# Five direct tiles instead of three, and input combinations on VectorE, in a seven-product feed-forward stage

## The chip, the cores and the metric

One core of one Trainium2 chip. The metric is the device time of one execution in microseconds (us); the kernel before has a median of 2582.3 us over 3 runs (2580.14 to 2583.24).

## The reference, cut to what matters

Four feed-forward stages (two layers, two in each) take most of the time. With `h` the normalised input (1024 features, 512 tokens) each computes

```python
def swiglu(h, w_gate, w_up, w_down):        # 1024 -> 2816 -> 1024
    return (jax.nn.silu(h @ w_gate) * (h @ w_up)) @ w_down
x = x + 0.5 * swiglu(rms_norm(x, norm), w_gate, w_up, w_down)
```

All of it is float32. The kernel gets that precision by splitting each operand into a high part, rounded to a short format (`fp32r`), and a low part (operand minus high part), and adds three products of parts: high by high, high by low, low by high.

## The kernel before

Everything is held with features on the 128 partitions and the 512 tokens along the free dimension, so `h` is 8 blocks of 128x512. The 2816 hidden features are 22 tiles of 128, numbered `f` = 0 to 21. `ffn` (line 340) runs `up(f)` for each tile, which gives the product of gate and up for those 128 features, split into `gh`/`gl`, and `down(k, ...)` for each of 8 output blocks and each chunk of tiles. `CHUNKS` puts the tiles 0 to 3 into the first chunk, 4 to 7 into the second, and so on. The 8 `down` calls of a chunk are spread over the tiles of the next: two after each `up`.

A tile is computed in one of two ways.

- **Direct** (`direct`, line 227; the tiles below `DIRECT`, here 0, 1 and 2): 8 blocks x 3 products of parts x 2 matrices = 48 matmuls of 512 columns on the unscaled input `xh`/`xl`; the result is multiplied by the normalisation factor `R` when it leaves PSUM (lines 238 and 241).
- **Seven products** (`winograd`, line 305; the tiles from 3 on): a scheme of Strassen's kind on 2x2 blocks, with 7 products of 256 columns instead of 8: 7 x 4 x 3 = 84 matmuls of 256 columns. It needs combinations of the weights (`blocks`, line 272: four sums, two on GpSimd and two on VectorE, then splits of seven 128x512 pieces, line 299 on ScalarE and line 300 on VectorE) and combinations of the scaled input (`forms`, line 244: once for each stage).

`forms` needs `R`, which is the broadcast of the input's norm (line 129, on VectorE) and comes late in the direct tiles. For each of four pairs of input blocks it scales two blocks on VectorE (line 253, into tiles `gh3`, `gl3`), makes four differences of 128x256 on GpSimd (line 260, into tiles of the tags `cu` and `s`, of which there are two each; `direct` and `winograd` put their own results `u` and `s` into the same tags), copies seven 128x256 high parts on ScalarE (line 267, `fh`) and subtracts for the low parts on VectorE (line 268, `fl`), in pieces of 256, 512, 512 and 512 columns.

What sets the order. The kernel is written in Tile. The order of each engine's instructions is fixed when the program is built: whenever an engine comes free in its own time model, a planner takes the instruction that stands earliest in the program among those that are ready there. `high_priority(offset=100)` around `weights` and `blocks` lets these count as 100 instructions earlier. `forms` is written between `up(0)` and `up(1)`; in the third stage, which follows the end of the first layer, `late` (lines 214 to 222) comes right behind it: a broadcast and eight scalings of `x` (line 220). A direct tile is 60 instructions. Tiles of one tag rotate through its buffers in program order, so a new one waits until the one that many places before is no longer used. The weights' raw data has two buffers (`raw`), their parts three each (`whi`, `wlo`); a direct tile takes two of each, a `down` one, a seven-product tile four of `whi`/`wlo`. Its raw blocks go into tiles that are free at the time: for `f` = 3 into `gh4` to `gl7`, for later ones into the slots of the input blocks `xh0` to `xl7`, which the direct tiles still read. PSUM has three banks of tag `s`, three of `t`, two of `acc`.

## Time and profile before

| | us |
|---|---|
| median of 3 runs | 2582.3 |
| the profiled execution | 2590.04 |
| its span, from the first to the last instruction | 2588.3 |
| busy: TensorE matmul / weight load | 2438.3 / 2114.6 |
| busy: VectorE / ScalarE / GpSimd | 1877.3 / 1293.1 / 814.9 |
| mean granted clock of TensorE | 0.970 |

The page gives busy time by engine and by line, the views of the trace each instruction with its start, its duration and what ended the idle time before it. PE is TensorE's matmuls, PEld its weight loads, DVE VectorE, ACT ScalarE, POOL GpSimd, SP the engine that issues the DMAs. A matmul's duration runs from its start to its modelled end and overlaps with the next, so the rate is read from the distance of two starts.

### The profile page before, as it was taken

To read this page: it belongs to the slowest core of one execution; us is meant where nothing else is said; L and a number is where in the kernel's file an instruction comes from. 1 tells how busy PE (TensorE), PEld (TensorE's weight loads), DVE (VectorE), ACT (ScalarE), POOL (GpSimd) and SP (SyncE) were. 2 spreads that over 40 slices of the span, in tenths; PEclk is the share of its full clock that TensorE was granted. 3 is DMA by queue.
4 is the path that set the end of the run, shared out by engine and by line. 5 is a ranking of instruction groups with operands and counts; after the bars stand their busy time and mean duration, and the time that the engine had idled before them with its cause. 6 is when DMAs were issued, how large, how long until landed. Compare 5 with 4: busy or idle time off the path is not lost. (4 is left out here: it accounts for less than half of the span.)

```text
span 2588.3 us, 40395 instructions
## 1 busy us (share of the span) xinstructions
PE 2438.3 (94%) x15192; PEld 2114.6 (82%) x15192; DVE 1877.3 (73%) x3307; ACT 1293.1 (50%) x2494; POOL 814.9 (31%) x647
## 2 busy tenths in 40 slices
PE   6999999999979999979999999999899998889998
PEld 5899988886669999769999888767799997777867
DVE  8877776976588777698777689755977766755444
ACT  4444456676444444544444576764444445334544
POOL 5212115652341111441211447224312104442312
PEclk8999999999989999989999999999899999999989
DMA  5233333211223332323332432012233324220111
GB/s 161 78 106 103 96 111 108 84 50 34 84 69 102 103 105 78 103 70 103 100 105 70 129 103 80 19 52 87 93 103 100 105 61 144 63 80 25 40 45 56
DMA packets 117284, 220.58 MB, mean 85 GB/s; under 512 B 22544, under 2 KB 33872, under 8 KB 117088
## 3 DMA queue, kind: packets, MB, share of 16 engines
q1 hardware_dynamic: 113680, 217.68, 27.7%
q8 instruction: 119, 1.95, 0.3%
q10 hardware_dynamic: 3408, 0.33, 0.1%
q14 instruction: 77, 0.63, 0.1%
HBM read 209.14 MB, written 8.78 MB: 84 GB/s over the span
## 5 line engine op out<-in xcount | busy, mean ns | idle before, releaser
L292 POOL TENSOR_TENSOR xl<-xh,xh 128x512 f32<-128x512 f32 x144 | 212.8, 1479 | 834.7 <-DVE wlo L300 458.9
L88 ACT ACTIVATE whi<-raw 128x512 fp32r<-128x512 f32 (+4 forms) x327 | 246.1, 754 | 433.5 <-PE t L317 222.4
L317 PE MATMUL t<-fl,whi 128*128 128x256 f32 x1216 | 342.6, 282 | 8.8 <-DVE fl L268 8.8
L317 PE MATMUL t<-fh,whi 128*128 128x256 f32 x1216 | 342.5, 282 | 6.2 <-ACT fh L267 6.2
L317 PE MATMUL t<-fh,wlo 128*128 128x256 f32 x1216 | 342.3, 281 | 1.0 <-DVE wlo L300 1.0
L99 PE MATMUL acc<-gh,whi 128*128 128x512 f32 x704 | 278.6, 397 | 7.8 <-DVE x L370 4.5
L317 PE MATMUL s<-fl,whi 128*128 128x256 f32 x912 | 258.9, 284 | 26.6 <-DVE fl L268 26.6
L101 PE MATMUL acc<-gh,wlo 128*128 128x512 f32 x704 | 278.1, 396 | 0.3
L100 PE MATMUL acc<-gl,whi 128*128 128x512 f32 x704 | 278.2, 396 | 0.0
L317 PE MATMUL s<-fh,whi 128*128 128x256 f32 x912 | 259.0, 284 | 11.4 <-ACT fh L267 8.4
L317 PE MATMUL s<-fh,wlo 128*128 128x256 f32 x912 | 257.1, 282 | 0.2 <-DVE wlo L300 0.2
L317 PEld LDWEIGHTS t<-fl,whi 128*128 128x128 f32 x1216 | 231.4, 190 | 16.1 <-DVE fl L268 9.8
L317 PEld LDWEIGHTS t<-fh,whi 128*128 128x128 f32 x1216 | 231.1, 190 | 13.5 <-ACT fh L267 7.0
L89 DVE TENSOR_TENSOR wlo<-raw,whi 128x512 fp32r<-128x512 f32 (+3 forms) x253 | 204.0, 807 | 50.4 <-ACT whi L88 49.6
L299 ACT ACTIVATE whi<-xh 128x512 fp32r<-128x512 f32 x216 | 136.7, 633 | 207.0 <-issue 113.3
L89 POOL TENSOR_TENSOR wlo<-raw,whi 128x1024 fp32r<-128x1024 f32 (+2 forms) x74 | 167.1, 2259 | 220.4 <-ACT whi L88 206.7
L317 PEld LDWEIGHTS t<-fh,wlo 128*128 128x128 f32 x1216 | 231.5, 190 | 1.4 <-DVE wlo L300 1.4
L300 DVE TENSOR_TENSOR wlo<-xh,whi 128x512 fp32r<-128x512 f32 x216 | 179.3, 830 | 33.3 <-ACT whi L299 33.2
L317 PEld LDWEIGHTS s<-fl,whi 128*128 128x128 f32 x912 | 174.0, 191 | 32.9 <-DVE fl L268 29.6
L299 ACT ACTIVATE whi<-xl 128x512 fp32r<-128x512 f32 x288 | 171.6, 620 | 57.2 <-PE t L317 48.7
L300 DVE TENSOR_TENSOR wlo<-xl,whi 128x512 fp32r<-128x512 f32 x288 | 192.9, 691 | 4.6 <-ACT whi L299 4.6
L317 PEld LDWEIGHTS s<-fh,whi 128*128 128x128 f32 x912 | 174.1, 191 | 17.8 <-ACT fh L267 10.3
(714 smaller groups left out, 6412.4 us busy)
## 6 DMA issues: line engine op xcount, KB each, us to landing
xh<-in_ffn_gu_dram SPq DMA_DIRECT2D x288, 256.0 KB, 2.6
raw<-in_ffn_d_dram SPq DMA_DIRECT2D x128, 256.0 KB, 2.6
raw<-in_w2f_dram SPq DMA_DIRECT2D x25, 512.0 KB, 3.6
raw<-in_ffn_gu_dram SPq DMA_DIRECT2D x24, 512.0 KB, 3.7
raw<-in_ffn_d_dram SPq DMA_DIRECT2D x64, 192.0 KB, 2.4
xs<-x SPq DMA_DIRECT2D x24, 256.0 KB, 2.6
raw<-in_a_dram SPq DMA_DIRECT2D x12, 512.0 KB, 3.5
x<-xs SPq DMA_DIRECT2D x24, 256.0 KB, 2.8
```

The lines of the kernel that those rows point to most:

```text
L88: nc.scalar.activation(out=hi, in_=raw, func=AF.Copy)
L89: (lo_eng or self.lo_eng).tensor_tensor(out=lo, in0=raw, in1=hi.bitcast(F32), op=ALU.subtract)
L99: mm(out=out, lhsT=lh, rhs=rh, start=start, stop=False)
L100: mm(out=out, lhsT=lh, rhs=rl, start=False, stop=False)
L101: mm(out=out, lhsT=ll, rhs=rh, start=False, stop=stop)
L292: eng.tensor_tensor(out=o, in0=x, in1=y, op=op)
L299: nc.scalar.activation(out=hi[:, c], in_=src, func=AF.Copy)
L300: nc.vector.tensor_tensor(out=lo[:, c], in0=src, in1=hi[:, c].bitcast(F32), op=ALU.subtract)
L317: nc.tensor.matmul(out=out, lhsT=x[:, k], rhs=y[:, j], start=start and k == 0 and n == 0, stop=stop and k == 3 and n == 2, skip_group_chec ...
```

## The change

`DIRECT` goes from 3 to 5: the whole first chunk and the first tile of the second are computed directly, and the first seven-product tile is `f` = 5. `forms` makes its four differences on VectorE, into one tile `W` of a new tag `tw` with one buffer, and splits them with one copy and one subtraction of 1024 columns; its two scaled blocks alternate between `gh7`/`gl7` and `gh4`/`gl4`. The raw blocks of the first seven-product tile come as two transfers of 512 KB into the tag `raw` instead of four of 256 KB into pool tiles, and its sums go into `gh5`, `gh6`, `gl5`, `gl6`. Each of the four stages' pools begins with a filler of 0, 8, 16 or 24 floats, so that all its tiles move up by 0, 32, 64 or 96 bytes.

```diff
@@ -56,7 +56,7 @@
         self.nc.sync.dma_start(out=t, in_=ap)
         return t
 
-    BUFS = dict(sqt=2, ms=4, hms=4, rs4=4, rs8=2, r12=2, s=2, cu=2, wu=2, nm=6, sum=6, rsum=6, cms=2, lms=2, lats=2,
+    BUFS = dict(sqt=2, ms=4, hms=4, rs4=4, rs8=2, r12=2, s=2, cu=2, wu=2, tw=1, nm=6, sum=6, rsum=6, cms=2, lms=2, lats=2,
                 beta=2, sq_=1, st=10, p=8, pth=3, ptl=3, vv=2, lat=6, ysq=2, c1=4, sums=3, frs=2, ft=2, fR=2, rr=1, y=4, dup=4, bias=1,
                 t3=4, t15=4, rt=1, kr=4, ahr=4, chr=4, hr=4, shift=2, tmp=3, n4=3, dense=2, L4=2, q4=3, t32t=2, UA=2, SA=2, ST=2, SG=1, yrw=1,
                 rest=2, sbt=3, rwms=2, sig=1, gate=1, oacc=8, fss1=4, fss=4, rs1=4, sums_=1)
@@ -246,26 +246,22 @@
 
         nc = self.nc
         out = []
+        lo, hi = slice(0, 256), slice(256, 512)
+        flat = lambda t: t.rearrange("p e c -> p (e c)")
+        sub = lambda o, x, y: nc.vector.tensor_tensor(out=o, in0=x, in1=y, op=ALU.subtract)
         for k in range(4):
-            hs = []
-            for j, tag in ((k, "gh3"), (k + 4, "gl3")):
-                h = self.t(gp, tag)
-                nc.vector.scalar_tensor_tensor(out=h, in0=self.x[j], scalar=gain[:, j:j + 1], in1=R, op0=ALU.mult, op1=ALU.mult)
-                hs.append(h)
-            a, b = hs
             H, L = self.t(gp, f"fh{k}", (P, 7, 256), F32R), self.t(gp, f"fl{k}", (P, 7, 256), F32R)
-            half = lambda t: t.rearrange("p (e c) -> p e c", e=2)
-            w0, w1 = half(self.t(gp, "cu")), half(self.t(gp, "s"))
-            lo, hi = slice(0, 256), slice(256, 512)
-            sub = lambda o, x, y: nc.gpsimd.tensor_tensor(out=o, in0=x, in1=y, op=ALU.subtract)
-            sub(w0[:, 0], a[:, hi], a[:, lo])
-            sub(w0[:, 1], b[:, hi], w0[:, 0])
-            sub(w1[:, 0], b[:, hi], a[:, hi])
-            sub(w1[:, 1], b[:, lo], w0[:, 1])
-            for j, src in ((0, half(a)[:, 0:1]), (1, half(b)), (3, w0), (5, w1)):
-                n = src.shape[1]
-                nc.scalar.activation(out=H[:, j:j + n], in_=src, func=AF.Copy)
-                nc.vector.tensor_tensor(out=L[:, j:j + n], in0=src, in1=H[:, j:j + n].bitcast(F32), op=ALU.subtract)
+            a, b = (self.t(gp, f"g{e}{7 - 3 * (k % 2)}") for e in "hl")
+            for j, o in ((k, a), (k + 4, b)):
+                nc.vector.scalar_tensor_tensor(out=o, in0=self.x[j], scalar=gain[:, j:j + 1], in1=R, op0=ALU.mult, op1=ALU.mult)
+            W = self.t(gp, "tw", (P, 4, 256))
+            sub(W[:, 0], a[:, hi], a[:, lo])
+            sub(W[:, 1], b[:, hi], W[:, 0])
+            sub(W[:, 2], b[:, hi], a[:, hi])
+            sub(W[:, 3], b[:, lo], W[:, 1])
+            for j, n, src in ((0, 1, a[:, lo]), (1, 2, b), (3, 4, flat(W))):
+                nc.scalar.activation(out=flat(H[:, j:j + n]), in_=src, func=AF.Copy)
+                sub(flat(L[:, j:j + n]), src, flat(H[:, j:j + n]).bitcast(F32))
             out.append((H, L))
         return out
 
@@ -274,17 +270,20 @@
 
         nc = self.nc
         with self.tc.high_priority(offset=self.ahead):
+            A = []
             if f == DIRECT:
-                slots = [(gp, f"g{t}{4 + i}") for t in "hl" for i in range(4)]
+                slot = iter([(gp, f"g{t}{i}") for t in "hl" for i in (5, 6)])
+                for which in range(2):
+                    t = self.wp.tile([P, 1024], F32, tag="raw", name=self.name("raw"), bufs=2)
+                    nc.sync.dma_start(out=t, in_=wgu[f, which])
+                    A += [t[:, 0:S], t[:, S:]]
             else:
-                slots = [(self.xp, f"x{t}{4 * (f % 2) + i}") for t in "hl" for i in range(4)]
-            slot = iter(slots)
-            A = []
-            for which in range(2):
-                for e in range(2):
-                    t = self.t(*next(slot))
-                    nc.sync.dma_start(out=t, in_=wgu[f, which][:, e * S:(e + 1) * S])
-                    A.append(t)
+                slot = iter([(self.xp, f"x{t}{4 * (f % 2) + i}") for t in "hl" for i in range(4)])
+                for which in range(2):
+                    for e in range(2):
+                        t = self.t(*next(slot))
+                        nc.sync.dma_start(out=t, in_=wgu[f, which][:, e * S:(e + 1) * S])
+                        A.append(t)
             a11, a12, a21, a22 = A
             s1, s2, s3, s4 = (self.t(*next(slot)) for _ in range(4))
             for eng, o, x, y, op in ((nc.gpsimd, s1, a21, a22, ALU.add), (nc.vector, s2, s1, a11, ALU.subtract),
@@ -341,6 +340,9 @@
 
         nc = self.nc
         with self.tc.tile_pool(name=self.name("ffn"), bufs=1, reuse_waits="tile") as gp:
+            pad = next(PAD)
+            if pad:
+                gp.tile([P, pad], F32, name=self.name("pad"))
             R = self.bcast(r, gp, "R", ACC)
             F = None
 
@@ -387,7 +389,8 @@
 
 
 CHUNKS = (0, 4, 8, 12, 16, 19, NFF)
-DIRECT = 3
+DIRECT = 5
+PAD = iter((0, 8, 16, 24))
 
 POOL = 'ac'
 COMB = (0, 1, 2)
```

## Rows read from the trace of the kernel before

**Rows 1.** The page: its span, and the matmul group with most waiting on forms.

```profile
span 2588.3 us, 40395 instructions
...
L317 PE MATMUL s<-fl,whi 128*128 128x256 f32 x912 | 258.9, 284 | 26.6 <-DVE fl L268 26.6
```

**Rows 2.** Stretches: from the last direct tile's end to the first down, four stages; then full work. Columns: stretch, length, busy us (instructions) of PE, PEld, DVE, ACT, POOL, clock, DMA share, GB/s.

```profile
46.88:88.00 41.12, 25.68 (x157) 22.74 (x156) 38.09 (x51) 16.86 (x32) 19.14 (x16) 0.71 0.19 61
750.02:783.57 33.55, 23.16 (x158) 22.07 (x157) 31.15 (x44) 14.45 (x27) 15.98 (x13) 0.75 0.23 72
1117.67:1159.44 41.77, 24.09 (x157) 21.13 (x156) 39.12 (x54) 16.14 (x30) 16.53 (x14) 0.75 0.19 61
1823.13:1856.46 33.33, 22.82 (x157) 21.47 (x156) 32.26 (x45) 14.57 (x27) 14.43 (x12) 0.80 0.22 73
76.00:370.00 294.00, 293.65 (x2028) 270.34 (x2027) 223.54 (x380) 133.83 (x250) 46.41 (x32) 1.00 0.32 93
```

**Rows 3.** Timeline of PE, first stage: first and last of 24, 60 and 12 matmuls.

```profile
41.44 0.39 PE L99 MATMUL t<-xh,whi 128*128 128x512 f32 x1
...
46.66 0.39 PE L101 MATMUL t<-xh,wlo 128*128 128x512 f32 x1
...
94.99 0.28 PE L317 MATMUL s<-fh,whi 128*128 128x256 f32 x1
...
101.88 0.28 PE L317 MATMUL s<-fh,wlo 128*128 128x256 f32 x1
...
103.86 0.40 PE L101 MATMUL acc<-gh,wlo 128*128 128x512 f32 x1
...
106.43 0.39 PE L100 MATMUL acc<-gl,whi 128*128 128x512 f32 x1
```

**Rows 4.** Timeline of DVE: where R is ready in each stage, and what follows.

```profile
35.26 0.69 DVE L129 COPY R<-acc 128x512 f32<-128x512 f32 x1 [1.97 <-PE acc L126]
...
731.14 0.69 DVE L129 COPY R<-acc 128x512 f32<-128x512 f32 x1 [0.61 <-PE acc L126]
...
1101.98 0.69 DVE L129 COPY R<-acc 128x512 f32<-128x512 f32 x1 [0.16 <-PE acc L126]
1102.70 0.69 DVE L238 TENSOR_TENSOR s<-s,R 128x512 f32<-128x512 f32 x1
1103.31 0.68 DVE L241 TENSOR_TENSOR cu<-t,R 128x512 f32<-128x512 f32 x1
1103.91 0.74 DVE L253 SCALAR_TENSOR_TENSOR gh<-x,gnext,R 128x512 f32<-128x512 f32 x1
...
1804.26 0.69 DVE L129 COPY R<-acc 128x512 f32<-128x512 f32 x1 [0.61 <-PE acc L126]
```

**Rows 5.** Single lines, ns min/median/max: low parts of forms, L220, weights' low parts, GpSimd's differences.

```profile
L268 DVE TENSOR_TENSOR fl<-gh,fh x16: 408/956/1480, 42.0 to 1830.1; 128x256 fp32r<-128x256 f32 x16
L268 DVE TENSOR_TENSOR fl<-s,fh x16: 676/680/1766, 46.5 to 1841.1; 128x512 fp32r<-128x512 f32 x16
...
L220 DVE SCALAR_TENSOR_TENSOR x<-x,fin_g,sqt x8: 739/1214/1774, 1107.3 to 1140.3; 128x512 f32<-128x512 f32 x8
...
L89 DVE TENSOR_TENSOR wlo<-raw,whi x4: 1216/1226/2305, 21.2 to 32.1; 128x1024 fp32r<-128x1024 f32 x4
...
L260 POOL TENSOR_TENSOR cu<-gh x16: 1046/1116/3257, 38.0 to 1826.9; 128x256 f32<-128x256 f32 x16
```

**Rows 6.** Stretches of the first stage around the clock's return (columns as in Rows 2).

```profile
71.00:73.00 2.00, 2.00 (x9) 2.00 (x10) 2.00 (x4) 1.47 (x4) 0.00 (x0) 0.50 0.01 4
...
75.00:77.00 2.00, 1.78 (x15) 1.78 (x16) 1.80 (x4) 1.21 (x3) 0.00 (x0) 1.00 0.05 15
```

**Rows 7.** Timelines of ACT and DVE: weights' parts around R, first and second stage.

```profile
35.95 0.63 ACT L299 ACTIVATE whi<-gh 128x512 fp32r<-128x512 f32 x1 [3.92 <-PE t L100]
...
735.55 1.75 DVE L89 TENSOR_TENSOR wlo<-raw,whi 128x1024 fp32r<-128x1024 f32 x1
...
768.14 0.68 DVE L268 TENSOR_TENSOR fl<-s,fh 128x512 fp32r<-128x512 f32 x1
```

**Rows 8.** The page's DMA issues: KB of each, us to landing.

```profile
raw<-in_ffn_gu_dram SPq DMA_DIRECT2D x24, 512.0 KB, 3.7
```

## The prediction

> **What bounds the kernel now.** I first read the page, then the stretches, then single instructions. TensorE is busy for nearly the whole span, and the waiting that stands on one group is on the operands that `forms` makes [rows 1]. The stretches show where: once a stage's seven-product tiles run, PE is busy without a break at full clock (the last row of [rows 2]), so there the number of matmuls and their distance set the time. Not so between the last direct tile and the first `down`: the four stages take 41.12, 33.55, 41.77 and 33.33 us for it, with VectorE busy for over nine tenths [rows 2].
>
> The distances of starts give the rates: 5.22/23 = 0.2270 us for a 512-column matmul of a direct tile, 6.89/59 = 0.1168 for a 256-column one of a seven-product tile, 2.57/11 = 0.2336 for a 512-column one of a `down` [rows 3]. So a direct tile costs 48 x 0.2270 = 10.90 us, a seven-product tile 84 x 0.1168 = 9.81, a `down` 12 x 0.2336 = 2.80. Each of the four stretches holds 156 seven-product matmuls besides the first of `down` [rows 2], 18.2 us at full speed. What is over is lost: 22.9, 15.3, 23.5 and 15.1 us, 77 us in all. The clock is part of that: after the gaps PE works at 0.50 (1.2 GHz), still so at 71 to 73 us without a break, and at 75 us at 1.00 [rows 6].
>
> **The change part by part.** I compare at one point: where seven-product tile 5 can begin, after tiles 3 and 4 and two `down`s. From there the program's work is the same in both kernels.
>
> *Before*, to that point: the stretch, then the rest of two `down`s and 12 matmuls of tile 4, 5.61 + 1.40 = 7.0 us. That is 48.1, 40.6, 48.8 and 40.3, together 177.8 us.
>
> *After, without any wait*: two direct tiles and two `down`s, 21.8 + 5.6 = 27.4 us, four times 109.6. So the new matmuls cost 2 x (10.90 - 9.81) = 2.2 us a stage more, and the largest gain is 177.8 - 109.6 = 68.2 us.
>
> *The wait that is left.* VectorE now does all of `forms`. Costs, by the distance of its starts: 512 columns 0.61 [rows 4], 0.08 less than the duration; by the same overlap 0.33 for 256 columns (0.408), 0.60 for 512 (0.676) and 1.14 for 1024 (1.216) [rows 5]; scaling a block 0.66 (0.74) [rows 4]. GpSimd's 1.1 us differences [rows 5] become VectorE ones of 0.33; none of before's VectorE rows is exactly that form (two float32 inputs in SBUF, float32 out), the nearest are line 268's, 0.408 undisturbed and 1.48 at worst. I take 0.33, since GpSimd, whose work stands beside the long ones, has none then. One quarter of `forms`: two scalings 1.32, four differences 1.32 and about 0.1 for the one that needs its predecessor, low parts 0.33 + 0.60 + 1.14, together 4.8; four quarters 19.3 us. The ScalarE copies (0.4 to 1.1 us) hide behind VectorE's next scalings; if that cover is gone, each quarter waits about 1 us more.
>
> Whether that hides under the two added tiles depends on the order. `forms` stands behind `up(0)`. The weights of tile 3 stand 120 instructions behind the end of `forms` and count as 100 earlier: still 20 behind. Before, `forms` often waited for GpSimd, and in such gaps VectorE took weights' parts, as at 735.55 [rows 7]. Now its next step is nearly always ready. So I expect that the low parts of tile 3's weights, whose buffer comes free early (35.95, [rows 7]), wait until `forms` is nearly through; matmuls of one bank keep their order, so PE stops at tile 3's third matmul of each bank. In the second and fourth stage the same holds for tile 2's second half (its low part comes behind `R` there, 735.55 [rows 7]), which counts as before the last quarter: the wait is then split, with the same sum.
>
> The wait per stage is then: end of `R` (start + 0.69, [rows 4]) + tile 0's four steps 2.4 + `forms` 19.3 + a gap of 0.3 (into the last of which the first weights' part falls), less the end of the direct tiles (left ends of [rows 2]); + 1.14 for tile 2's part in stages two and four; + 0.6 + 8 x 0.66 = 5.9 for `late` in stage three [rows 5]. That is 35.95 + 22.0 - 46.88 = 11.1; 731.83 + 23.1 - 750.02 = 4.9; 1102.67 + 27.9 - 1117.67 = 12.9; 1804.95 + 23.1 - 1823.13 = 4.9. Together 33.8 us. Each drops the clock; I take some 4 us at half speed, as from 71 to 75 us [rows 6], 2 us lost, 8 in all. Behind that VectorE has room: the other parts of tiles 3 and 4, their way out of PSUM and tile 5's own 5.4 us make some 15 us against 27.
>
> *Tile 5's weights.* `raw` is now shared by tiles 3 and 4, the two `down`s and tile 5, so its second half is fetched only when the second `down`'s raw data is split, which needs a `whi` buffer that tile 4's first half gives back. That is about 9 us ahead of the need; landing takes 3.7 [rows 8], GpSimd's first sum, the VectorE one and the splits some 4. SP issues in order: the loads of tile 6 and of later `down`s queue behind these two. I take 1 us a stage, between 0 and 3.
>
> *The fillers.* The stage's tiles move by 32, 64 and 96 bytes in stages two to four. Direct tiles read the input from other pools at 0.2270, `down` from this pool at 0.2336 [rows 3]; whether the address makes that difference no row shows. If a shift wins it back, 528 `down` matmuls a stage gain 0.0066 each, 3.5 us, 10.4 in three; if it costs half as much on each of 17 x 84 256-column ones, it loses 4.7, 14 in three. I take 0 and keep both ends.
>
> Sum: 109.6 + 33.8 + 8 + 4 = 155.4 against 177.8: 22 us less. The profiled execution of 2590.04 (its span 2588.3 and 1.7 around it) would become 2568; it lies 0.3% above the median of the runs, and the same 22 us off 2582.3 give 2560.
>
> One rule of the Trainium skill bears on the price of a VectorE step. First the rows: a 512-column low part takes 676 ns undisturbed and up to 1766 beside GpSimd's work, a GpSimd difference 1046 to 3257 [rows 5]. "SBUF — State Buffer", section "SBUF: two separate sides", says that GpSimd and a VectorE operation with two SBUF inputs take an exclusive lock on a shared pair of ports and that the loser waits for a whole instruction. The rows agree with it. By it, all that `forms` lost to GpSimd's differences is gone, as in the sum; priced with the disturbed rows instead (1.5 for 256 columns, 1.8 for 512), a quarter would be over 10 us and nothing of the gain would be left. On the fillers, section "Operand start alignment" of that page states legality only and says that speed was not timed; no run here shows more.
>
> **The rivals.**
>
> *The weights get between.* If the planner finds gaps in `forms`, the low parts of tiles 3 and 4 slip in and `forms` is done later, under the 27 us. VectorE's work from `R` to tile 5's start is then 2.4 + 19.3 + four weights' parts 4.6 + two tiles' ways out 4.8 + 1.2 for the `down`s + 2.4 for tile 5's first pieces = 34.7, which ends at 23.8, 16.5, 25.6 (with `late`) and 16.5 us behind the direct tiles' end, within 27.4. For: it happened before (735.55). Against: the gaps before were GpSimd's. It gains 45 to 65 us: 2525 typically.
>
> *The hand-offs set the pace.* Before, `forms` took from `R` at 731.8 to 768.8 in stage two [rows 4, 7], 9 us a quarter, with only 3.5 of its own VectorE work in each. If the chain scaling, ScalarE copy, VectorE subtraction through a single `W`, with other work queued between, and not VectorE's work, keeps the quarter long, tile 3 waits for all of it. Each us more per quarter costs 16 us; from 4.8 + 22/16 = 6.2 us a quarter on the change is slower. At 7.3 it would be 2582.3 - 22 + 40 = 2600. For: the pace measured, and a lone buffer of `tw` where there were two each. Against: most of that pace was GpSimd's 4 x 1.1 us and the seven-product tiles' weights, both gone from there.
>
> *The gain is eaten elsewhere.* The fillers at their bad end (14) and tile 5's weights at theirs (3 a stage, 8 more) make 22: no change, 2582. For: neither has a row. Against: both must hit.
>
> *No work moved at all* is no case: the counts of matmuls follow from the code.
>
> **How the numbers follow.** Forecast 52%, 2560 (2550 to 2570 with the fillers' ends); weights between 20%, 2525; pace 15%, 2600; eaten 13%, 2582. 0.2%, about what a measurement of this kernel can tell from no change, is 5 us. Faster: nearly all of the first two and a little of the rest, 0.71; within: most of the last, 0.13; slower: the pace and the edge of the last, 0.16. The range leaves out the better half of the second case and two thirds of the third: 2530 to 2588.
>
> **What would show it.** In the profile after: 17 x 84 x 4 = 5712 matmuls on the seven-product line; `forms` within about 20 us of `R`, at 4.8 us a quarter, with VectorE's 256-column steps near 0.41; a wait of PE at tile 3's low parts (tile 2's in stages two and four) of 11, 5, 13 and 5 us, ended by the weights' subtraction and not by `forms`; no wait of tile 5; the same 0.2336 and 0.1168 in all four stages. Wrong would make it: no wait at tile 3 (then 2525), waits on `forms` in tile 5 (the pace), other distances in stages two to four (the fillers).

## The result, and the profile after

The change makes the kernel 1.1% faster: 2552.8 us (2550.6 to 2561.6, four runs) against 2582.6 (2580.1 to 2583.2) of before; the ratio is 0.9893, 95% interval 0.9868 to 0.9918. That is 29.9 us off the median; the forecast was 22 off, 2560. The sign and the size came true. The way did not: of the costs in the sum the largest, the wait at tile 3, fell to nothing; tile 5's weights, put at 4 us, made PE wait for 18; and an experiment below shows that the order of work which the forecast had assumed would have made the kernel slower.

The page of after (its profiled execution took 2554.3 us, span 2552.4): for one bank of the seven-product matmuls the busy time, and the idle time before them with what ended most of it.

```profile
L316 PE MATMUL s<-fh,whi 128*128 128x256 f32 x816 | 231.5, 284 | 11.3 <-ACT whi L298 6.0
L316 PE MATMUL s<-fh,wlo 128*128 128x256 f32 x816 | 231.7, 284 | 9.3 <-DVE wlo L299 9.3
L316 PE MATMUL s<-fl,whi 128*128 128x256 f32 x816 | 230.8, 283 | 1.1 <-DVE fl L251 1.1
```

The 26.6 us that one group waited for `fl` [rows 1] are 1.1 now. Most of what is left stands on weights, `whi` and `wlo`. Three operands times (1088 + 816) are 5712 matmuls, as the code says.

Stretches of after (columns as in [rows 2]): 28 us of each stage that end with the direct tiles and the two `down`s, and then tile 5 up to its first 60 matmuls (72 and two of a `down` in the first stage).

```profile
46.00:74.00 28.00, 28.00 (x125) 23.06 (x124) 25.81 (x40) 12.04 (x17) 3.15 (x2) 1.00 0.47 147
737.00:765.00 28.00, 28.00 (x125) 23.14 (x124) 22.35 (x36) 10.35 (x14) 2.92 (x3) 1.00 0.46 146
1096.00:1124.00 28.00, 28.00 (x124) 23.09 (x123) 26.61 (x42) 10.93 (x17) 3.42 (x3) 1.00 0.44 142
1797.00:1825.00 28.00, 28.00 (x125) 23.07 (x124) 21.73 (x36) 10.34 (x14) 2.15 (x2) 1.00 0.46 146
...
74.46:95.04 20.58, 14.20 (x76) 12.82 (x74) 15.84 (x23) 6.43 (x11) 6.17 (x4) 0.67 0.19 59
765.17:779.27 14.10, 9.33 (x62) 8.62 (x61) 14.10 (x20) 5.11 (x9) 6.22 (x4) 0.88 0.26 72
1124.95:1147.71 22.76, 13.04 (x61) 11.35 (x60) 19.28 (x28) 7.32 (x11) 4.82 (x4) 0.63 0.15 45
1825.40:1839.99 14.59, 10.19 (x61) 9.62 (x60) 14.59 (x20) 5.10 (x9) 6.72 (x4) 0.77 0.24 72
```

PE is busy for all 28 us of the first four, at a clock of 1.00: there is no wait at tile 3, none at tile 2, and the point "tile 5 can begin" is reached in the time of the matmuls alone. All the loss has moved behind it. At 0.1168 us each, 60 matmuls are 7.0 us, and 72 with two of a `down` are 8.9: tile 5 loses 20.6 - 8.9 = 11.7, then 14.1 - 7.0 = 7.1, 15.8 and 7.6, together 42 us, the slow clock (0.63 to 0.88) included. Before lost 77 by the forecast's reading of [rows 2]. Of the 42, 25 are waits of over 0.1 us: 18 on `whi` and `wlo`, 4.5 on `fh` and `fl` (in stages one and three alone), 2.7 on `wu`, a VectorE step on the way out of tile 5. The other 17 are matmuls that came further apart than 0.1168, most of them while the clock was down.

The order of VectorE shows why tile 3 does not wait. Its timeline in the first stage of after (start, length; R's copy is at 34.57):

```profile
39.75 0.68 DVE L241 TENSOR_TENSOR cu<-t,R 128x512 f32<-128x512 f32 x1
40.34 1.22 DVE L89 TENSOR_TENSOR wlo<-raw,whi 128x1024 fp32r<-128x1024 f32 x1
41.48 0.42 DVE L251 TENSOR_TENSOR tw<-gh 128x256 f32<-128x256 f32 x1
...
45.23 0.42 DVE L251 TENSOR_TENSOR tw<-gl,tw 128x256 f32<-128x256 f32 x1
45.57 1.22 DVE L89 TENSOR_TENSOR wlo<-raw,whi 128x1024 fp32r<-128x1024 f32 x1
```

The low parts of the direct tiles' weights (L89) stand between the steps of `forms`, not behind them: a difference that needs its predecessor, or a low part that needs ScalarE's copy, leaves a place, and the planner filled it. The order is the trace's; that it was such places that let the weights in is read from it. So PE is never short up to tile 5, and `forms` is late instead.

**Where the 29.9 us are.** One stage is read from the start of R's copy ([rows 4] for before) to the start of its last `down` matmul.

| us | stage 1 | 2 | 3 | 4 | sum |
|---|---|---|---|---|---|
| before | 346.2 | 347.0 | 351.3 | 348.2 | 1392.7 |
| after | 338.2 | 339.3 | 349.0 | 345.6 | 1372.1 |
| last low part of `forms` behind R, before | 36.4 | 37.7 | 41.5 | 37.5 | |
| the same, after | 53.2 | 40.5 | 59.6 | 40.5 | |

The stages give 20.6 us, against 22 in the sum. The mix stretches between a last `down` and the next R are 349.7 and 351.0 us before, 346.3 and 347.6 after: 6.8 us that the forecast had not looked for. The stretch behind the last stage was 8.2 us shorter in this execution; the experiments show that this varies by itself.

### The profile page after: what moved, and what is told of

Read it like the earlier page. It is cut to its first block, busy times and chain, and to the rows that moved or that the text cites. A ratio compares the mean times of both kernels' runs of the same rounds, so it can differ in the third digit from the quotient of the medians.

```text
span 2552.4 us, 39475 instructions
## 1 busy us (share of the span) xinstructions
PE 2437.3 (95%) x14904; PEld 2108.9 (83%) x14904; DVE 1832.3 (72%) x3275; ACT 1270.1 (50%) x2422; POOL 718.4 (28%) x567
## 5 line engine op out<-in xcount | busy, mean ns | idle before, releaser
L88 ACT ACTIVATE whi<-raw 128x1024 fp32r<-128x1024 f32 (+4 forms) x343 | 263.1, 769 | 480.1 <-PE t L316 208.8
L316 PE MATMUL t<-fh,wlo 128*128 128x256 f32 x1088 | 308.5, 284 | 2.1 <-DVE wlo L299 2.1
L316 PE MATMUL t<-fh,whi 128*128 128x256 f32 x1088 | 308.0, 283 | 1.5 <-ACT fh L263 0.8
L316 PE MATMUL t<-fl,whi 128*128 128x256 f32 x1088 | 307.6, 283 | 0.0
L89 DVE TENSOR_TENSOR wlo<-raw,whi 128x512 fp32r<-128x512 f32 (+3 forms) x269 | 220.3, 819 | 51.0 <-ACT whi L88 50.1
L316 PE MATMUL s<-fh,whi 128*128 128x256 f32 x816 | 231.5, 284 | 11.3 <-ACT whi L298 6.0
L316 PE MATMUL s<-fh,wlo 128*128 128x256 f32 x816 | 231.7, 284 | 9.3 <-DVE wlo L299 9.3
L316 PE MATMUL s<-fl,whi 128*128 128x256 f32 x816 | 230.8, 283 | 1.1 <-DVE fl L251 1.1
L89 POOL TENSOR_TENSOR wlo<-raw,whi 128x1024 fp32r<-128x1024 f32 (+2 forms) x74 | 167.1, 2260 | 220.7 <-ACT whi L88 207.2
L316 PEld LDWEIGHTS t<-fh,whi 128*128 128x128 f32 x1088 | 207.5, 191 | 8.2 <-ACT whi L298 1.1
L316 PEld LDWEIGHTS t<-fl,whi 128*128 128x128 f32 x1088 | 208.0, 191 | 6.2
L372 DVE SCALAR_TENSOR_TENSOR x<-acc,x 128x512 f32<-128x512 f32 x184 | 126.5, 687 | 76.1 <-PE acc L101 75.9
```

The costliest lines, as they stand in the source:

```text
L88: nc.scalar.activation(out=hi, in_=raw, func=AF.Copy)
L89: (lo_eng or self.lo_eng).tensor_tensor(out=lo, in0=raw, in1=hi.bitcast(F32), op=ALU.subtract)
L316: nc.tensor.matmul(out=out, lhsT=x[:, k], rhs=y[:, j], start=start and k == 0 and n == 0, stop=stop and k == 3 and n == 2, skip_group_chec ...
L372: nc.vector.scalar_tensor_tensor(out=x, in0=ps, scalar=0.5, in1=x, op0=ALU.mult, op1=ALU.add)
```

## The experiments

The median of before differs a little between the chips (2584.0 beside e0 to e3, 2589.3 beside e4 to e6 and e8, 2585.7 beside e7, e9, e11 and e12), so kernels of different groups are compared by their ratio to before. "Stages" is the sum over the four stages as in the table above; it is free of what varies outside them. It comes from one execution of each kernel, and two executions of before differ in it by 5.7 us (e0): a smaller difference is not told apart by it alone.

| run | direct tiles | differences on | fillers, bytes | last low part behind R | stages | median | ratio to before (95%) |
|---|---|---|---|---|---|---|---|
| before | 3 | GpSimd | none | 36.4, 37.7, 41.5, 37.5 | 1392.7 | | |
| after | 5 | VectorE | 0, 32, 64, 96 | 53.2, 40.5, 59.6, 40.5 | 1372.1 | 2552.8 | 0.9893 (0.9868, 0.9918) |
| e1 | 5 | VectorE | none | 53.4, 40.5, 58.8, 40.5 | 1367.3 | 2549.6 | 0.9874 (0.9849, 0.9900) |
| e2 | 5 | GpSimd | as after | 38.7, 36.5, 45.9, 36.5 | 1366.8 | 2554.4 | 0.9887 (0.9860, 0.9915) |
| e3 | 3 | VectorE | as after | 42.8, 44.1, 49.2, 44.2 | 1431.2 | 2608.0 | 1.0101 (1.0075, 1.0127) |
| e5 | 3 | VectorE, old buffers | none | 35.2, 36.2, 41.0, 36.2 | 1389.3 | 2577.6 | 0.9973 (0.9950, 0.9997) |
| e7 | 5 | VectorE, weights held | none | 30.0, 31.4, 35.7, 31.5 | 1430.8 | 2613.5 | 1.0103 (1.0071, 1.0135) |
| e9 | 3 | VectorE, split unjoined | as after | 41.0, 43.4, 47.7, 43.4 | 1424.1 | 2603.7 | 1.0067 (1.0043, 1.0092) |
| e11 | 5 | VectorE, half buffers | none | 52.1, 37.9, 58.7, 37.9 | 1359.5 | 2542.3 | 0.9823 (0.9800, 0.9847) |

**e0: the kernel before, a second time.** No edit.

> The kernel before, profiled a second time. Nothing is changed. Its profiled execution of 2590.04 us lay 7.5 above its median, and between the profiles of before and after 15.5 us stand in code that the change does not touch: each of the two mix stretches is 3.5 us shorter in after, the stretch behind the last stage 8.3. Theory (one execution differs from the next): this profile is near 2582, its two mix stretches come out some 2 us shorter each and the tail some 4 us shorter, while the four stages keep their 346.1, 347.1, 351.2 and 348.1 us within 1 us. Rival (the untouched stretches really gained, since the stages hand something over earlier): they stay at 349.7, 351.1 and 435.9 within 1 us, and the 7.5 us lie elsewhere.

This execution took 2594.1 us, with stages of 347.5, 347.1, 351.6 and 352.0 (1398.3 in all, against 1392.7), mix stretches of 350.4 and 350.2, and 425.7 from the last `down` to the kernel's last matmul (426.8 in the first profile). The fourth stage is 3.8 us longer, 2.3 of them at its start: from 37.7 to 45.7 us behind R its granted clock was 0.57, where the first profile had 0.96. Near 2582 it did not come. The mix stretches keep their length, as the rival had it; in e5, which has the form of before, they are 350.6 and 351.1, in the kernels made from the changed one 346.0 to 349.6, most of them near 347, with three direct tiles as with five. So some 3 us a stretch seem to belong to the change; what hands them over stays open. The last stretch is another matter: 415.8 in e5, which has the form of before, and 412.4 (e6) to 428.6 (e1) among the kernels made from the changed one. It tells nothing of the change.

**e3: three direct tiles, VectorE.**

```
-DIRECT = 5
+DIRECT = 3
```

> The changed kernel with three direct tiles, as in before: VectorE makes the input combinations, but the cover of the two added direct tiles is gone. The matmuls fall back by 2.2 us a stage. Theory (VectorE is faster, but its work cannot be hidden under three tiles): the forms end about 25 us behind R, the direct tiles end 11 to 19 us behind it, and tile 3 waits about 15 us in stages one and three, about 8 to 10 in two and four, against 23 and 15 lost in before: a gain of 15 to 30 us on before, 2553 to 2567. Rival (the pace of a quarter is set by hand-offs, not by the engine): forms as slow as before, 2575 to 2585. If the cover were the whole of the gain, this kernel would be no faster than before.

2608 us: slower than before by 1.0%, where the theory had 2553 to 2567 and the rival 2575 to 2585. Both fell; what was said last, that without the cover there might be no gain at all, came true. With the cover gone, the new `forms` is worse than the old, and its last low part is 6 to 8 us later. PE waits at tile 3, second stage:

```profile
764.66 0.58 PE L316 MATMUL s<-fh,whi 128*128 128x256 f32 x1 [10.10 <-ACT fh L263]
```

and VectorE, which has nothing else by then, shows the chain:

```profile
772.83 1.22 DVE L251 TENSOR_TENSOR fl<-tw,fh 128x1024 fp32r<-128x1024 f32 x1 [1.12 <-ACT fh L263]
774.09 0.43 DVE L251 TENSOR_TENSOR tw<-gh 128x256 f32<-128x256 f32 x1
774.43 0.42 DVE L251 TENSOR_TENSOR tw<-gl,gh 128x256 f32<-128x256 f32 x1
774.77 0.88 DVE L251 TENSOR_TENSOR tw<-gl,tw 128x256 f32<-128x256 f32 x2
776.76 1.22 DVE L251 TENSOR_TENSOR fl<-tw,fh 128x1024 fp32r<-128x1024 f32 x1 [1.12 <-ACT fh L263]
```

Four differences, 1.12 us of waiting for one ScalarE copy of 1024 columns, one subtraction, and only then the first difference of the next quarter, since `tw` has one buffer: 776.76 - 772.83 = 3.9 us a quarter, with scalings and the first low parts not even in it.

**e2: five direct tiles, GpSimd's differences.**

```
-            sub(W[:, 0], a[:, hi], a[:, lo])        (and the other three)
+            psub(W[:, 0], a[:, hi], a[:, lo])       psub: the same on nc.gpsimd
```

> The changed kernel, but the four differences of a quarter of the input combinations are done by GpSimd, as in before; the five direct tiles, the joined splits and the fillers stay. Theory (what counts is the cover of two more direct tiles, and the engine matters through the port that it shares with VectorE): a quarter takes 7 to 9 us again, the forms end some 36 us behind R, where the direct tiles end 33.5 to 40.6 us behind it, so tile 5 waits 4 to 8 us longer in stages one and three and little longer in stages two and four: 10 to 20 us above after, 2563 to 2573. Rival A (the engine does not matter once the cover is there): 2553 within 3. Rival B (VectorE, slowed by GpSimd, also delays the weights of the direct tiles, so that these wait): 2585 or more.

2554.4 us, the time of after; Rival A. `forms` ends 14.5, 4, 13.7 and 4 us earlier with GpSimd than with VectorE in the same kernel. Waits of PE in the first stage of e2, 60 to 110 us, and in the third, 1100 to 1160 (us in total, times, longest):

```profile
PE t L317 <- DVE wlo L300: 3.6, 1, 3.6
PE s L317 <- ACT whi L299: 2.5, 1, 2.5
...
PE t L317 <- DVE wlo L300: 5.1, 1, 5.1
PE t L317 <- ACT whi L299: 2.9, 1, 2.9
```

`fh` and `fl` are not in these lists any more (two waits of 0.5 and 0.6 us on other weights are left out): the combinations are ready, and tile 5 waits for its own weights. So the gain needs the two added direct tiles and does not need the move to VectorE: with them it brings nothing, and without them the rest of the change (VectorE, one buffer, joined split, shared `raw`, fillers) costs 1%. Five direct tiles alone, with everything else as before, were not run.

**e5: before, with only the engine changed.**

```
-            sub = lambda o, x, y: nc.gpsimd.tensor_tensor(out=o, in0=x, in1=y, op=ALU.subtract)
+            sub = lambda o, x, y: nc.vector.tensor_tensor(out=o, in0=x, in1=y, op=ALU.subtract)
```

> The kernel before with one word changed: the four differences of each quarter of the input combinations are done by VectorE in place of GpSimd; three direct tiles, two buffers for the differences and four splits a quarter stay. It tells apart why the run with three direct tiles and VectorE was 24 us slower than before, with the last low part 42.8, 44.1, 49.2 and 44.2 us behind the start of R against 36.4, 37.7, 41.5 and 37.5. Theory A (VectorE is the full engine here, and 5.3 us of differences more, in its order, come on top): the last low part at +41 to +45, as late as there, about 2600 to 2610. Theory B (the single buffer and the joined split made the chain: differences, one ScalarE copy, one subtraction, then only the next quarter): the last low part at +34 to +38, 2570 to 2585. In between would say that both have a part.

2577.6 us, ratio 0.9973: Theory B. VectorE alone is no loss, rather a small gain (0.9950 to 0.9997), and the last low part comes 0.5 to 1.5 us earlier than with GpSimd. So it is not the load of VectorE that made e3 slow. The forecast had put the long `forms` of before down to "GpSimd's 4 x 1.1 us and the seven-product tiles' weights". The first of the two can be left out: without GpSimd's differences the four quarters are 0.5 to 1.5 us shorter in all.

**e9: e3 with the split unjoined.**

```
-            for j, n, src in ((0, 1, a[:, lo]), (1, 2, b), (3, 4, flat(W))):
+            for j, n, src in ((0, 1, a[:, lo]), (1, 2, b), (3, 2, flat(W[:, 0:2])), (5, 2, flat(W[:, 2:4]))):
```

> Three direct tiles, the combinations on VectorE, one buffer for the four differences as in the change, but their high and low parts are made in two steps of two differences each, as in the kernel before, not in one joined step of four. The joined one with three direct tiles took 2608 (24 above before), the last low part at +42.8, 44.1, 49.2 and 44.2 us behind the start of R; the kernel before with only the engine changed, with two buffers and two steps, 2578, at +35.2, 36.2, 41.0 and 36.2. Theory (the joined step is the chain: nothing of a quarter's differences can be copied until the fourth is there, and the next quarter waits for the last subtraction): here +35 to +38 and 2575 to 2588. Rival (the single buffer is the chain, the steps do not matter): +42 to +49 and 2600 to 2610. Half way, some 2592, says that both have a part.

2603.7 us, and +41 to +48: the rival, nearly whole. VectorE in the last two quarters of e9, second stage:

```profile
769.47 0.88 DVE L251 TENSOR_TENSOR tw<-gl,tw 128x256 f32<-128x256 f32 x2
770.58 1.29 DVE L251 TENSOR_TENSOR fl<-tw,fh 128x512 fp32r<-128x512 f32 x2 [0.24 <-ACT fh L263]
...
772.59 0.88 DVE L251 TENSOR_TENSOR tw<-gl,tw 128x256 f32<-128x256 f32 x2
773.70 1.29 DVE L251 TENSOR_TENSOR fl<-tw,fh 128x512 fp32r<-128x512 f32 x2 [0.24 <-ACT fh L263]
```

The chain shortens from 3.9 to 3.1 us a quarter, yet the last low part moves by 0.7 to 1.8 us only. The joined step is the smaller part. The rest of the distance to e5 (some 24 us by the ratios) goes with what e5 still has of before: two buffers for the differences, one pair of tiles for the scaled blocks, tile 3's raw blocks in tiles of their own, and no fillers (some 5 us, by e1 below). These were not tried apart. In e9 every wait of PE over 0.1 us from the end of the direct tiles to 50 us behind R ends on `fh` or `fl`, none on a weight, so it is not tile 3's blocks that PE waits for; that it is the buffer is argued from the chain, not shown.

**e7: the order that the forecast had assumed.**

```
+                self.last = sub(flat(L[:, j:j + n]), src, flat(H[:, j:j + n]).bitcast(F32)).ins
...
+        with self.tc.issue_after(self.last) if self.hold else nullcontext():     (hold: tile 3)
             (lo_eng or self.lo_eng).tensor_tensor(out=lo, in0=raw, in1=hi.bitcast(F32), op=ALU.subtract)
```

> The changed kernel without fillers, and on VectorE's queue the low parts of tile 3's weights stand behind the last split of the input combinations. This is the order that the forecast had assumed and that the changed kernel does not have: there the weights' parts came in between, tiles 3 and 4 ran without a wait, and the combinations ended 53.4, 40.5, 58.8 and 40.5 us behind the start of R. Theory (the price in the forecast was right, only the order was not): here the last low part is at +23 to +29, PE stops at tile 3's low parts for 11, 5, 13 and 5 us and hardly at tile 5: 34 us and a slower clock behind each, less some 20 that tile 5 no longer loses: 2560 to 2575. Rival A (the combinations take longer than 4.8 us a quarter even with VectorE for themselves, since differences, one ScalarE copy and one subtraction form a chain through one buffer): the last low part at +30 or later, waits of 17 us and more at tile 3 in stages one and three: 2585 to 2600. Rival B (the order does not matter, PE waits as long in either place): 2549.

2613.5 us, 1.0% slower than before. PE at tile 3's first low part, in the four stages:

```profile
65.23 0.79 PE L102 MATMUL s<-xh,wlo 128*128 128x512 f32 x1 [17.59 <-DVE wlo L90]
768.10 0.79 PE L102 MATMUL s<-xh,wlo 128*128 128x512 f32 x1 [12.69 <-DVE wlo L90]
1153.04 0.80 PE L102 MATMUL s<-xh,wlo 128*128 128x512 f32 x1 [20.77 <-DVE wlo L90]
1857.23 0.79 PE L102 MATMUL s<-xh,wlo 128*128 128x512 f32 x1 [12.70 <-DVE wlo L90]
```

17.6, 12.7, 20.8 and 12.7, together 64 us, where the forecast had 11.1, 4.9, 12.9 and 4.9. The wait, its place and its releaser are those that the forecast described; its size was half. VectorE ended `forms` 30.0 us behind R in the first stage, not 22.4. Its timeline there shows 7.0 of these 7.6: the ways out of tiles 1 and 2 (eight steps of 0.6 us, 4.8) came among `forms`, where the forecast had counted tile 0's alone, and twice the 1.12 us of the ScalarE copy that e3 shows, which it had called hidden. At 7.3 us a quarter it had put 2600; here R to the last low part, less the copy and tile 0's way out, is 6.7 a quarter. Up to tile 5 the four stages are 74 us behind e1: the 64 of the wait, and 10 of matmuls further apart behind it, for which the forecast had 8 (the clock). Tile 5 still waits some 3 us a stage for a low part of its weights; by its first 60 matmuls it loses 31 us in all, where e1 loses 42.

**e1 and e4: the fillers.**

```
-PAD = iter((0, 8, 16, 24))
+PAD = iter((0, 0, 0, 0))          e1
+PAD = iter((8, 4, 12, 40))        e4
```

> The changed kernel with all four fillers at 0. Theory (where the stage's tiles lie sets the distance of matmuls): stages three and four go back from 0.1200 and 0.1183 to 0.1168 us a seven-product matmul, which is 4.9 and 2.7 us less, and stage two loses what its 32 bytes gave, 0.1152 to 0.1168 and 0.2290 to 0.2334, some 2 to 4 us more: together about 4 us less than after, near 2549. Rival (the distances differ between executions, or by what else runs then, not by the address): the four stages differ among themselves as they do in after, and the time is that of after, 2553. A third outcome, slower than after by over 5 us, would say that the fillers pay.

> The changed kernel with other fillers: 32, 16, 48 and 160 bytes in the four stages, in place of 0, 32, 64 and 96. Theory (the distance of matmuls follows the address of the stage's tiles within 128 bytes): stage one, at 32 bytes, takes the distances that stage two of the changed kernel had, a `down` at 0.229 to 0.230 in place of 0.2334 and a seven-product matmul at 0.115 to 0.117 in place of 0.1168, and is some 4 us shorter; stage four, at 160, which is 32 beyond 128, does the same in place of 0.1184 and is some 5 us shorter than in after; 16 and 48 bytes are new, between 0.115 and 0.120. Stage three loses its 0.1200 unless 48 is as bad. Together 5 to 14 us below after: 2539 to 2548. Rival A (the sum of the bytes counts, not the remainder): stage four at 160 bytes keeps 0.118 or more. Rival B (the stage, not the address, makes the distances of stage two): stage one stays at 0.1168 and 0.2334.

First and last of 60 seven-product matmuls in one go: the third stage of after (64 bytes), of e1 (none), the fourth of e4 (160 bytes).

```profile
1171.89 0.28 PE L316 MATMUL s<-fh,whi 128*128 128x256 f32 x1
...
1178.97 0.28 PE L316 MATMUL s<-fh,wlo 128*128 128x256 f32 x1
```

```profile
1176.03 0.28 PE L316 MATMUL s<-fh,whi 128*128 128x256 f32 x1
...
1182.92 0.28 PE L316 MATMUL s<-fh,wlo 128*128 128x256 f32 x1
```

```profile
1861.15 0.28 PE L316 MATMUL s<-fh,whi 128*128 128x256 f32 x1
...
1867.84 0.28 PE L316 MATMUL s<-fh,wlo 128*128 128x256 f32 x1
```

7.08, 6.89 and 6.69 us over 59 steps: 0.1200, 0.1168 and 0.1134. Without fillers all four stages have 0.1168 and 0.2334 again, and the stages together are 4.8 us shorter than in after (the medians, 2549.6 and 2552.8, do not separate the two). So the fillers of the change cost some 5 us; one execution's stages do not show that, but the distances do: a tile with its two `down`s comes every 15.40 us without a shift in all four stages of e1, and in after every 15.40, 15.28, 15.68 and 15.56, which is 5 us over 16 tiles. e4 took 2545.1 us, ratio 0.9827 (0.9778, 0.9876), its stages 338.5, 337.7, 347.7 and 339.7: stage two (16 bytes) is 5.7 us shorter than in e1, stage four (160) 2.4, stage three (48) 4.5 longer, with the 0.1200 of 64 bytes. Stage one, at 32 bytes, is only half as expected: `down` at 0.229, but the seven-product stretches at 0.118, above the 0.1168 without a shift, and the stage gains nothing. The total came where it was expected, by other stages than expected. Rival A falls in stage four, which gained although 160 is the largest shift, and so does Rival B for `down`, which did change in stage one. But the remainder of 128 does not settle it either: 32 and 160 differ.

**e6 and e8: tile 5's weights early.** Both without fillers; e8 has GpSimd's differences.

```
-                    t = self.wp.tile([P, 1024], F32, tag="raw", name=self.name("raw"), bufs=2)
-                    nc.sync.dma_start(out=t, in_=wgu[f, which])
+                for which, i in ((0, 5), (0, 6), (1, 5), (1, 6)):
+                    t = self.t(gp, f"g{'hl'[which]}{i}")
+                    with self.tc.high_priority(offset=160):
+                        nc.sync.dma_start(out=t, in_=wgu[f, which][:, (i - 5) * S:(i - 4) * S])
...
+                s1, s2, s3, s4 = self.t(gp, "gh7"), self.t(gp, "gl7"), w[:, 0:S], w[:, S:]     (w: a tile of tag tw)
```

> The changed kernel without fillers, and tile 5's weights on another way: its four blocks are loaded at the start of the stage into four tiles of the stage that are free until tile 5's own output needs them, and the sums stand in two tiles that the input combinations have left and in the buffer of the differences. Nothing else. The kernel without fillers loses at tile 5's start 3.4 and 3.7 us in stages two and four on the second operand's low part, and more in one and three. Theory (tile 5 waits for its late weights in stages two and four, and for weights and input combinations in one and three, where the last low part is at +53 and +59): in stages two and four tile 5 loses about 1 us, in one and three half of what it lost; 10 to 16 us below the kernel without fillers, 2533 to 2540. Rival A (the weights' way is covered by the input combinations): 2549. Rival B (the early loads take bandwidth from the direct tiles' weights, or the buffer of the differences is free too late): 2549 to 2560.

> The same early weights of tile 5, no fillers, and the four differences of a quarter on GpSimd, so that the last low part of the input combinations stands at +36 to +46 us behind R in place of +40 to +59. Theory (with GpSimd's differences tile 5 waits for its weights alone, 24 us in the four stages together: 6.7, 5.7, 8.6 and 4.1): these go, all but 1 us a stage, and the time is 2526 to 2532. Rival A (GpSimd's sums of tile 5's weights now come behind its differences and are as late as before): 2545 to 2550. Rival B (early loads hurt): 2550 or more. If this kernel and the one with the differences on VectorE are the same within 3 us, the engine of the differences does not matter even without late weights.

The reason for them is in after. PE's waits in tile 5, stages two and three:

```profile
770.31 0.38 PE L316 MATMUL s<-fh,wlo 128*128 128x256 f32 x1 [3.09 <-DVE wlo L299]
777.75 0.39 PE L316 MATMUL s<-fh,whi 128*128 128x256 f32 x1 [1.65 <-DVE wu L319]
...
1131.03 0.58 PE L316 MATMUL s<-fh,whi 128*128 128x256 f32 x1 [4.25 <-ACT whi L298]
...
1141.01 0.58 PE L316 MATMUL s<-fh,whi 128*128 128x256 f32 x1 [2.54 <-ACT fh L263]
```

and ahead of them, first stage, SP's queue and GpSimd's:

```profile
64.29 3.73 SPq L285 DMA_DIRECT2D xh<-in_ffn_gu_dram  x6
68.12 0.38 SPq L278 DMA_DIRECT2D raw<-in_ffn_gu_dram  x1
```

```profile
70.63 1.85 POOL L291 TENSOR_TENSOR xl<-xh,xh 128x512 f32<-128x512 f32 x1 [0.38 <-DMA xh<-in_ffn_gu_dram]
74.48 1.59 POOL L291 TENSOR_TENSOR gh<-raw 128x512 f32<-128x512 f32 x1 [2.00 <-DMA raw<-in_ffn_gu_dram]
```

The second half of tile 5's weights is issued at 68.12, behind six loads for the next tiles, and lands at 74.4, when PE could begin. In the other stages two to four loads stand ahead of it; there it lands 2 to 3 us before PE could begin, 5.8 to 6.4 us behind its issue, where the first half took 3.5. Behind the landing VectorE's steps are longer beside GpSimd's sums, second stage:

```profile
763.41 1.77 DVE L291 TENSOR_TENSOR gh<-gh,raw 128x512 f32<-128x512 f32 x1 [2.26 <-POOL gh L291]
766.82 1.76 DVE L291 TENSOR_TENSOR gl<-raw,gh 128x512 f32<-128x512 f32 x1
```

These two, and one between them, take 1.77 us each with GpSimd at work, 0.68 without. That is 3.3 us more ahead of the low part for which PE then waits 3.09; whether PE would wait without it was not tried.

e6 took 2548.7 us, ratio 0.9835 (0.9792, 0.9877), stages 1363.4: 3.9 us less than e1 there, a third of what was expected, and less than two executions of before differ by (5.7). Tile 5 now waits 1 to 3 us for the low part of its third product and for `wu`, and in stages one and three still for `forms` (+51.8 and +55.6). Rival A holds for the most part: behind the late weights stood the late combinations, and behind both VectorE's order.

e8 took 2537.1 us, ratio 0.9797 (0.9758, 0.9835), stages 1356.2. GpSimd's differences are better than VectorE's here by 11.6 us in the median, on the same chip, and by 7.2 in the stages; with four runs each, of 2538.6 to 2554.7 and 2533.6 to 2543.5, the size is loose and the two intervals overlap. So the engine of the differences may matter once the weights are early, and then for GpSimd. It falls short of 2526 to 2532 for this reason, on VectorE in the second stage:

```profile
758.24 0.68 DVE L304 TENSOR_TENSOR wlo<-gl,whi 128x512 fp32r<-128x512 f32 x1
763.76 0.69 DVE L296 TENSOR_TENSOR xl<-xl,xh 128x512 f32<-128x512 f32 x1 [4.85 <-POOL xl L296]
```

and GpSimd and PE beside it:

```profile
762.44 1.29 POOL L296 TENSOR_TENSOR xl<-xh,xh 128x512 f32<-128x512 f32 x1 [0.98 <-DMA xh<-in_ffn_gu_dram]
768.73 0.58 PE L321 MATMUL t<-fh,wlo 128*128 128x256 f32 x1 [4.28 <-DVE wlo L304]
```

VectorE stands at a sum for tile 6, whose data is still on the way (GpSimd's sum before it waits for the transfer until 762.44), while tile 5's next low part is queued behind it; PE then waits 4.28 us for that, up to 768.73.

**e11 and e12: what came out fastest.** e11 is e1 with two half-size buffers and no joined split; e12 is e8 with an earlier place for tile 5's sums and with other fillers; inside that place its four loads count as 60 earlier, 160 in e8.

```
-            W = self.t(gp, "tw", (P, 4, 256))
+            w0, w1 = (self.t(gp, "tw", (P, 2, 256)) for _ in range(2))                  e11 (tw=2)
-        with self.tc.high_priority(offset=self.ahead):
+        with self.tc.high_priority(offset=200 if f == DIRECT else self.ahead):          e12
+PAD = iter((4, 40, 4, 40))                                                              e12
```

> The changed kernel without fillers, with the buffer of the differences cut into two halves of half the size, each with its own split (no joined step). Five direct tiles stay. Theory (with five direct tiles the chain is hidden in stages two and four, where tile 5 waits for weights, and shows in one and three, where the last low part is at +53 and +59 and tile 5 waits for it at +52 to +56): the last low parts come earlier by 4 to 8 us, stages one and three gain 2 to 4 us each, the others nothing: 2541 to 2547 against 2549.6 of the kernel without fillers. Rival A (all hidden, or the other work of VectorE takes the room): 2549. Rival B (more instructions on the full engine): 2552 or more.

> The kernel with early weights of tile 5 and GpSimd's differences, and two more edits: tile 5's sums and splits count as 200 instructions earlier in the order (100 before), and fillers of 16, 160, 16 and 160 bytes. In that kernel tile 5 still lost 4.6, 6.4 and 3.4 us in stages two to four at its third product, because VectorE stood 4.85 us at a sum for tile 6, which waited for a transfer, ahead of tile 5's splits. Theory: these waits go (10 to 14 us), and the fillers bring 2 to 5 us a stage, as 16 bytes did in stage two and 160 in stage four (0.1149 and 0.1140 us a seven-product matmul against 0.1168): 2510 to 2522 where that kernel had 2537. Rival A (the fillers' effect belongs to the stage or the program and not to the bytes): 2523 to 2530, with other distances than these. Rival B (the waits stay, since something else of tile 5 is late): 2527 or more.

e11: 2542.3 us, ratio 0.9823 against 0.9874 of e1, and stages 7.8 us shorter than e1's, 3.7, 2.2, 1.5 and 0.4 of it in the four; that is what was expected in sum, but the last low part moved by 2.6 us in stages two and four and by 1.3 and 0.1 in one and three, so not by the way that was expected; which way it was stays open. e12: 2532.3 us, ratio 0.9782 (0.9754, 0.9810), the lowest of all, though not told apart from e8's 0.9797 by the ratios. The earlier place did nothing: in the second stage VectorE again stands 4.99 us, up to 760.85, at the sum for tile 6, as in e8. What it gains on e8 in the stages (1343.8 against 1356.2; 3.7, 4.3, 0 and 4.4 in the four) is the fillers: 160 bytes give 0.1134 to 0.1138 in both of its stages, as in e4; 16 bytes give 0.1133 in the long stretches of the first stage and 0.118 in the third, where nothing is gained. So Rival B holds for the place (the waits stay), and for 16 bytes Rival A.

## Why the prediction was right, and where it was not

The total was near by luck: errors cancelled. The sum had 45.8 us of loss behind the matmuls (33.8 + 8 + 4), nearly all of it at tile 3; the runs show 42 at tile 5, none at tile 3, and 5 for the fillers. All three signs that the forecast named for being wrong were there: no wait at tile 3, waits on `forms` in tile 5, other distances in stages two to four.

- *What bounds the kernel, and the largest gain* (77 us lost before, 2.2 us a stage for the new matmuls): right. From the pieces as measured, 77 - 42 - 8.8 - 5 for the fillers = 21, and the stages show 20.6.
- *The wait at tile 3, 33.8 us, and 8 for the clock behind it*: wrong. It was nothing. The step that failed is "now its next step is nearly always ready": the chain difference, ScalarE copy, subtraction through one buffer is not always ready, and the weights' parts got between, with the differences on VectorE as they had with GpSimd's (e7 shows what the assumed order costs). That is the second case of the forecast, put at 20%, and its sign for it (no wait at tile 3) was there. Its price was not: it had `forms` done under the 27 us, and in stages one and three it ended 53 and 60 us behind R, where tile 5 could begin at 40 and 42.
- *A quarter of `forms` at 4.8 us, the ScalarE copies hidden*: too small. With only the ways out of tiles 1 and 2 between (e7) it is 6.7, of which these are 1.2 and the waits for ScalarE's copy 0.6; in after, with weights between, 9 to 14. The durations of single steps were right (0.42, 0.68, 1.22 us); the sum of durations was not the length, since a chain and other tiles' steps lie between. This is the rival "the hand-offs set the pace", which had its turning point at 6.2 us a quarter. With the forecast's order (e7) it did decide, and the kernel was slower than before, at 2613 more than the 2591 that the rival's own price gives for 6.7; in after the order took its force. The forecast held a long `forms` and a harmless `forms` for alternatives; they came together.
- *Tile 5's weights, 1 us a stage, between 0 and 3*: mis-sized, with the range too. PE waits 3.1 to 5.9 us a stage for them, 18 in all, and with the waits on `fh`, `fl` and `wu` and the slow clock tile 5 loses 42. "About 9 us ahead of the need" holds in stages two and four; in one and three the issue is 6.3 and 7.7 us ahead. "Landing takes 3.7" does not hold: it takes 5.8 to 6.4, with loads for the next tiles just ahead and behind. And "the splits some 4" left out VectorE's and GpSimd's other work there, and that VectorE's steps take 1.77 us beside GpSimd's sums. The text counted what queues behind these loads and not what stands ahead.
- *Fillers at 0, ends -10 to 14*: inside, at about +5. That the address might set the distance was rightly left open.
- *GpSimd's load as the cause of the slow `forms` of before*: wrong in what follows from it. The rows showed VectorE's steps beside GpSimd at up to 1766 ns [rows 5]. The rule of the Trainium skill, "SBUF — State Buffer", section "SBUF: two separate sides", that the one that comes second waits for the other's whole instruction, agrees with that. But the long `forms` did not hang on such steps: with the differences on VectorE and all else as before it ended 0.5 to 1.5 us sooner (e5), and in the kernel of five direct tiles 4 to 14.5 us sooner with GpSimd's than with VectorE's (e2). That GpSimd's run beside VectorE's other work explains the second, but is argued.
- *Outside the stages* nothing was forecast; 6.8 us came in the mix stretches, most of what the 29.9 have over the 20.6.

## What to carry to other kernels

The length of a chain of small steps on an engine that works in order is set by what the planner puts between them and, as far as e5 and e9 tell, by how many buffers the chain passes through, not by the sum of its steps; price it from the trace's own pace, and ask separately whether anything waits for its end. When a change bundles more cover for a late operand with a faster way to make it, test them apart: here the gain came with the cover, and the rest of the change was a loss without it. When a total comes out near the forecast, look at its terms: here none of the three terms of the loss was. When an operand's wait goes, look at once at what the next tile needs, from the issue of its loads on, and at everything queued ahead of each step.

## What the runs showed of the hardware that was not expected

The distance of matmuls depends on where the stage's tiles begin. A 256-column one took 0.1168 us without a shift in every stage of before, e1 and e8; 0.1200 with 48 and 64 bytes, 0.118 to 0.1185 with 96, 0.1134 to 0.1138 with 160. With 16 and 32 bytes it was 0.113 in some programs and stages and 0.118 in others, in some (after's second stage) one in the short and the other in the long stretches; a `down` came to 0.229 to 0.230 there, against 0.2334. A tile and its two `down`s take 15.40 us without a shift; 48 and 64 bytes cost 0.28 us, 96 cost 0.16, 160 gave 0.28, and 16 and 32 gave 0 to 0.25. At equal bytes the program and the stage make a difference, so the filler's bytes are not the whole rule; which other address it is measured against was not found.
